# A row softmax on one core: 16-row tiles, four-row blocks in a fixed order, and stores from ScalarE's queue

## The chip, the cores and the metric

The kernel runs on one core of a Trainium2 chip. The metric is device time in microseconds (us), lower is better. One run in the profiler gives the trace; its span (first to last instruction) is about 2 us shorter than the measured time. Engines are named as in the profile: DVE is VectorE, ACT is ScalarE, POOL is GpSimd, SP is SyncE; a trailing q (ACTq) is an engine's sequencer, which hands work to the engine and issues DMAs. The input is 33.55 MB, the output is 33.55 MB.

## The reference

```python
x = np.random.randn(16, 1024, 512).astype(np.float32)

def reference(x):
    x_scaled = x / 0.5
    x_max = np.max(x_scaled, axis=-1, keepdims=True)
    exp_x = np.exp(x_scaled - x_max)
    return (exp_x / np.sum(exp_x, axis=-1, keepdims=True)).astype(np.float32)
```

That is 16384 independent softmaxes of 512 numbers each, after a multiplication by 2.

## The kernel before

A tile is 128 partitions by `G = 8` rows of 512 numbers (2 MB); there are 16 tiles and 8 buffers. The tile is changed in place and stored. The order of instructions on each engine is left to the framework's scheduler.

```python
G = 8
N_ACT_NORM = 2
xr   = xf.rearrange("(c p g) d -> c p g d", p=P, g=G)
outr = of.rearrange("(c p g) d -> c p g d", p=P, g=G)
data  = ctx.enter_context(tc.tile_pool(name="data", bufs=8))
stats = ctx.enter_context(tc.tile_pool(name="stats", bufs=8))

for c in range(C):                                   # C = 16
    xt = data.tile([P, G, D], fp32, name="xt")
    nc.sync.dma_start(out=xt, in_=xr[c])                              # L44, load
    nc.vector.reduce_max(negmax, xt, axis=AX, negate=True)            # L47
    for g in range(G):
        nc.scalar.activation(out=xt[:, g, :], in_=xt[:, g, :], func=EXP,   # L51
                             bias=negmax[:, g : g + 1], scale=2.0,
                             accum_out=sums[:, g : g + 1])
    nc.vector.reciprocal(recip, sums)                                 # L61
    k = N_ACT_NORM
    nc.vector.tensor_mul(xt[:, k:, :], xt[:, k:, :],                  # L65, six rows
                         recip[:, k:].unsqueeze(2).broadcast_to((P, G - k, D)))
    for g in range(N_ACT_NORM):                                       # L71, two rows
        nc.scalar.activation(out=xt[:, g, :], in_=xt[:, g, :], func=COPY,
                             scale=recip[:, g : g + 1])
    nc.gpsimd.dma_start(out=outr[c], in_=xt)                          # L78, store
# ... allocations of the small tiles and the launch are cut
```

The bias is `-max(x)` and not `-2 max(x)`; the constant cancels in the division.

The softmax here doesn't subtract the row's maximum and nothing guards it: scores larger than these inputs give would overflow.

Of the kernel before, what the change touches and what calls it, by code (L numbers as in the profile page):

```python
# [1 line left out]

# [4 lines left out]


@with_exitstack  # L10
def kernel(
    ctx: ExitStack,
    tc: tile.TileContext,
    x: bass.AP,
    out: bass.AP,
):
    nc = tc.nc
    fp32 = mybir.dt.float32
    P = nc.NUM_PARTITIONS

    D = x.shape[-1]
    xf = x.flatten_outer_dims()
    of = out.flatten_outer_dims()
    N = xf.shape[0]

    G = 8
    C = N // (P * G)
    assert C * P * G == N

    N_ACT_NORM = 2  # L30

    xr = xf.rearrange("(c p g) d -> c p g d", p=P, g=G)
    outr = of.rearrange("(c p g) d -> c p g d", p=P, g=G)

    data = ctx.enter_context(tc.tile_pool(name="data", bufs=8))
    stats = ctx.enter_context(tc.tile_pool(name="stats", bufs=8))

    AX = mybir.AxisListType.X
    EXP = mybir.ActivationFunctionType.Exp
    COPY = mybir.ActivationFunctionType.Copy  # L40

    for c in range(C):
        xt = data.tile([P, G, D], fp32, name="xt")
        nc.sync.dma_start(out=xt, in_=xr[c])  # L44

        negmax = stats.tile([P, G], fp32, name="negmax")
        nc.vector.reduce_max(negmax, xt, axis=AX, negate=True)  # L47

        sums = stats.tile([P, G], fp32, name="sums")
        for g in range(G):  # L50
            nc.scalar.activation(  # L51
                out=xt[:, g, :],
                in_=xt[:, g, :],
                func=EXP,
                bias=negmax[:, g : g + 1],
                scale=2.0,
                accum_out=sums[:, g : g + 1],
            )

        recip = stats.tile([P, G], fp32, name="recip")  # L60
        nc.vector.reciprocal(recip, sums)  # L61

        if N_ACT_NORM < G:
            k = N_ACT_NORM
            nc.vector.tensor_mul(  # L65
                xt[:, k:, :],
                xt[:, k:, :],
                recip[:, k:].unsqueeze(2).broadcast_to((P, G - k, D)),
            )
        for g in range(N_ACT_NORM):  # L70
            nc.scalar.activation(  # L71
                out=xt[:, g, :],
                in_=xt[:, g, :],
                func=COPY,
                scale=recip[:, g : g + 1],
            )

        nc.gpsimd.dma_start(out=outr[c], in_=xt)  # L78


# [1 line left out]
_INS = ['x']  # L82
_OUTS = [((16, 1024, 512), 'float32')]


# [23 lines left out]
```

## Time and profile before

| | before |
|---|---|
| time, median of 3 runs | 164.66 us (164.35 to 164.81) |
| span of the profiled run | 162.7 us |
| busy: DMA queues q1 + q0, DVE, ACT | 97.5%, 77%, 69% |
| rate in a steady stretch | 431 GB/s |

These are lines of the page of the kernel before: busy time per engine; the span in 40 slices of 4.07 us (DMA busy in tenths, and what the DMA engines moved); the DMA queues (packets, MB, share of the 16 DMA engines); and the costliest groups of instructions (busy us and mean ns of one, then the idle time before them).

```profile
span 162.7 us, 483 instructions
DVE 124.6 (77%) x48; ACT 112.5 (69%) x289; POOL 8.8 (5%) x20
DMA  5999999999999999999999999999999999979994
GB/s 161 431 431 427 431 439 334 411 433 443 423 423 443 431 419 443 439 415 439 443 411 433 443 423 423 443 431 419 439 443 415 435 443 415 431 318 447 407 431 193
q1 hardware_dynamic: 2304, 33.56, 49.2%
q0 software_dynamic: 2304, 33.56, 48.3%
q14 instruction: 2, 0.02, 0.0%
...
L51 ACT ACTIVATE xt<-xt,negmax 128x512 f32<-128x512 f32 x128 | 90.5, 708 | 28.3 <-DVE negmax L47 28.3
L47 DVE TENSOR_REDUCE negmax<-xt 128x8 f32<-128x4096 f32 x16 | 70.5, 4406 | 25.6 <-DMA xt<-in_x_dram 25.6
L65 DVE TENSOR_TENSOR xt<-xt,recip 128x3072 f32<-128x3072 f32 x16 | 53.6, 3349 | 0.1
```

The DMA engines are the only ones that work all the time. DVE and ACT have idle time, and what ends it is a load (DVE) or DVE (ACT). The rate is flat except in four places: the first slice, slice 7 (334 GB/s), slice 36 (318 GB/s), and the last. While the bytes and the steady rate stay the same, they are the only time that a change can win.

The view of stretches gives the same for chosen stretches of the kernel before (from:to and length in us, busy us and instructions of DVE, ACT and POOL, clock, DMA share, GB/s):

```profile
core 0: us, DVE busy (x) ACT busy (x) POOL busy (x), PEclk, DMA share, GB/s
24.40:28.50 4.10, 4.10 (x3) 2.98 (x8) 0.00 (x0) 1.00 1.00 332
48.00:136.00 88.00, 71.67 (x29) 66.63 (x173) 5.32 (x10) 1.00 1.01 431
142.00:146.50 4.50, 4.47 (x3) 4.50 (x13) 0.53 (x1) 1.00 0.82 350
146.50:152.00 5.50, 4.71 (x3) 2.73 (x6) 0.53 (x1) 1.00 0.95 396
```

The second dip is at 142 to 152 us. The timeline of DVE and of POOL's store issues, kernel before (start us, length us, engine, line, what; in brackets the idle time before it and what ended it):

```profile
134.36 0.20 DVE L61 RECIPROCAL recip<-sums 128x8 f32<-128x8 f32 x1
136.47 4.42 DVE L47 TENSOR_REDUCE negmax<-xt 128x8 f32<-128x4096 f32 x1 [1.91 <-DMA xt<-in_x_dram]
140.80 3.35 DVE L65 TENSOR_TENSOR xt<-xt,recip 128x3072 f32<-128x3072 f32 x1
...
134.99 0.53 POOL L78 DMA_DIRECT2D out_dram<-xt  x1 [9.18 <-ACT xt L51]
144.69 0.53 POOL L78 DMA_DIRECT2D out_dram<-xt  x1 [9.17 <-ACT xt L51]
```

At 134.36 us DVE has the reciprocals of tile 13 (counting from 0) and could multiply. But its next instruction is the reduction of tile 15, which waits 1.9 us for that tile's load and takes 4.4 us. The multiply starts at 140.80, and tile 13's store is issued at 144.69, 9.7 us after the one before. A 2 MB store alone takes about 4.9 us, so with the loads over the queue runs dry. While loads still run, they fill the same gap.

### The profile page before, as it was taken

To read this page: it belongs to the slowest core of one execution; us is meant where nothing else is said; L and a number is where in the kernel's file an instruction comes from. 1 tells how busy PE (TensorE), PEld (TensorE's weight loads), DVE (VectorE), ACT (ScalarE), POOL (GpSimd) and SP (SyncE) were. 2 spreads that over 40 slices of the span, in tenths; PEclk is the share of its full clock that TensorE was granted. 3 is DMA by queue.
4 is the path that set the end of the run, shared out by engine and by line. 5 is a ranking of instruction groups with operands and counts; after the bars stand their busy time and mean duration, and the time that the engine had idled before them with its cause. 6 is when DMAs were issued, how large, how long until landed. Compare 5 with 4: busy or idle time off the path is not lost.

```text
span 162.7 us, 483 instructions
## 1 busy us (share of the span) xinstructions
DVE 124.6 (77%) x48; ACT 112.5 (69%) x289; POOL 8.8 (5%) x20
## 2 busy tenths in 40 slices
DVE  0098799999999979596993959969596895999200
ACT  0038997999999995939589294885939579396000
POOL 0000010010101010101001010010101001011100
DMA  5999999999999999999999999999999999979994
GB/s 161 431 431 427 431 439 334 411 433 443 423 423 443 431 419 443 439 415 439 443 411 433 443 423 423 443 431 419 439 443 415 435 443 415 431 318 447 407 431 193
DMA packets 4610, 67.13 MB, mean 413 GB/s; under 512 B 512, under 2 KB 512, under 8 KB 512
## 3 DMA queue, kind: packets, MB, share of 16 engines
q1 hardware_dynamic: 2304, 33.56, 49.2%
q0 software_dynamic: 2304, 33.56, 48.3%
q14 instruction: 2, 0.02, 0.0%
HBM read 33.55 MB, written 33.55 MB: 413 GB/s over the span
## 4 chain that ended last, share of the span: by engine, by line
DMA 61%; DVE 18%; ACT 8%; issue 6%; POOLq 0%; SPq 0%
DMA xt<-in_x_dram 40%; DMA out_dram<-xt 22%; DVE negmax L47 11%; ACT xt L51 7%; DVE xt L65 6%; ACT xt L71 1%; DVE recip L61 0%; POOLq L104 0%; SPq L44 0%; POOLq L78 0%
## 5 line engine op out<-in xcount | busy, mean ns | idle before, releaser
L51 ACT ACTIVATE xt<-xt,negmax 128x512 f32<-128x512 f32 x128 | 90.5, 708 | 28.3 <-DVE negmax L47 28.3
L47 DVE TENSOR_REDUCE negmax<-xt 128x8 f32<-128x4096 f32 x16 | 70.5, 4406 | 25.6 <-DMA xt<-in_x_dram 25.6
L65 DVE TENSOR_TENSOR xt<-xt,recip 128x3072 f32<-128x3072 f32 x16 | 53.6, 3349 | 0.1
L51 ACT ACTIVATION_READ_ACCUMULATOR xt<-xt,negmax 128x1 f32 x128 | 24.0, 187 | 0.0
L71 ACT ACTIVATE xt<-xt,recip 128x512 f32<-128x512 f32 x32 | 21.1, 707 | 0.3 <-DVE recip L61 0.3
L78 POOL DMA_DIRECT2D out_dram<-xt x16 | 8.6, 540 | 143.5 <-ACT xt L51 89.3
L51 ACT ACT_TABLE_LOAD x1 | 1.3, 1283 | 8.4 <-DMA xt<-in_x_dram 8.4
L61 DVE RECIPROCAL recip<-sums 128x8 f32<-128x8 f32 x16 | 3.1, 195 | 1.2 <-ACT xt L51 1.2
L93 POOL MEMSET const-float32-0.0<- 128x1 f32 x1 | 0.1, 98 | 0.2 <-issue 0.2
L93 POOL MEMSET const-bfloat16-1.0<- 128x1 bf16 x1 | 0.1, 101 | 0.0
L93 POOL MEMSET const-float32-1.0<- 128x1 f32 x1 | 0.1, 98 | 0.0
L93 POOL MEMSET const-uint8-127<- 128x1 uint8 x1 | 0.1, 98 | 0.0
## 6 DMA issues: line engine op xcount, KB each, us to landing
xt<-in_x_dram SPq DMA_DIRECT2D x16, 2048.0 KB, 28.8
out_dram<-xt POOLq DMA_DIRECT2D x16, 2048.0 KB, 17.0
```

The lines of the kernel that those rows point to most:

```text
L47: nc.vector.reduce_max(negmax, xt, axis=AX, negate=True)
L51: nc.scalar.activation(out=xt[:, g, :], in_=xt[:, g, :], func=EXP, bias=negmax[:, g : g + 1], scale=2.0, accum_out=sums[:, g : g + 1],)
L61: nc.vector.reciprocal(recip, sums)
L65: nc.vector.tensor_mul(xt[:, k:, :], xt[:, k:, :], recip[:, k:].unsqueeze(2).broadcast_to((P, G - k, D)),)
L71: nc.scalar.activation(out=xt[:, g, :], in_=xt[:, g, :], func=COPY, scale=recip[:, g : g + 1],)
L78: nc.gpsimd.dma_start(out=outr[c], in_=xt)
L93: nc = _bacc.Bacc("TRN2", target_bir_lowering=False, num_devices=1)
```

## The change

Its intent: bigger transfers; compute that starts early, in blocks of four rows, with the stages of successive blocks in a fixed order on each engine; a multiply with one tensor source on DVE; no GpSimd in the loop. The core of the diff, with allocations cut:

```diff
-    G = 8
+    G = 16
+    B = 4
+    N_ACT = 1
-    N_ACT_NORM = 2
-    data = ctx.enter_context(tc.tile_pool(name="data", bufs=8))
+    FIRST = [(0, 4), (4, 16)]                       # tile 0 comes in two loads
+    data = ctx.enter_context(tc.tile_pool(name="data", bufs=6))
+    ctx.enter_context(tc.manual_schedule())         # order as written
+    nc.vector.memset(warm, 0.0)
+    nc.scalar.activation(out=warm, in_=warm, func=EXP)   # primes the table
...
-        nc.vector.reduce_max(negmax, xt, axis=AX, negate=True)
+        nc.vector.tensor_reduce(negmax, xb, axis=AX, op=MAX, negate=True)   # xb: 4 rows
+        nc.vector.tensor_scalar_mul(bias, negmax, 2.0)
...
-            nc.vector.tensor_mul(xt[:, k:, :], xt[:, k:, :], recip[:, k:]...broadcast)
+        for g in range(B - N_ACT):
+            nc.vector.tensor_scalar_mul(xb[:, g, :], xb[:, g, :], recip[:, g : g + 1])
...
-        nc.gpsimd.dma_start(out=outr[c], in_=xt)
+        if b + B == G:
+            nc.scalar.dma_start(out=outr[c], in_=tiles[c])
...
+    for i in range(n + 3):                          # n = 32 blocks
+        if i < n:
+            if blocks[i][1] == 0:
+                load(blocks[i][0])
+            shift(i)                                # DVE: reduce, double
+            exponentials(i)                         # ACT
+        if 1 <= i <= n:
+            scale_vector(i - 1)                     # DVE: reciprocal, 3 multiplies
+        if 2 <= i <= n + 1:
+            scale_scalar(i - 2)                     # ACT: 1 COPY
+        if 3 <= i:
+            store(i - 3)                            # ACT's queue, once per tile
```

More of the change, by code (lines that the diff above doesn't have):

```diff
@@ L19 @@
     P = nc.NUM_PARTITIONS
+    AX = mybir.AxisListType.X
+    EXP = mybir.ActivationFunctionType.Exp
+    COPY = mybir.ActivationFunctionType.Copy
+    MAX = mybir.AluOpType.max
     D = x.shape[-1]
@@ L24, with load, shift, exponentials @@
     N = xf.shape[0]
-    G = 8
+    G = 16
+    B = 4
+    N_ACT = 1
     C = N // (P * G)
     assert C * P * G == N
-    N_ACT_NORM = 2
     xr = xf.rearrange("(c p g) d -> c p g d", p=P, g=G)
     outr = of.rearrange("(c p g) d -> c p g d", p=P, g=G)
-    data = ctx.enter_context(tc.tile_pool(name="data", bufs=8))
-    stats = ctx.enter_context(tc.tile_pool(name="stats", bufs=8))
-    AX = mybir.AxisListType.X
-    EXP = mybir.ActivationFunctionType.Exp
-    COPY = mybir.ActivationFunctionType.Copy
-    for c in range(C):
-        xt = data.tile([P, G, D], fp32, name="xt")
-        nc.sync.dma_start(out=xt, in_=xr[c])
-        negmax = stats.tile([P, G], fp32, name="negmax")
-        nc.vector.reduce_max(negmax, xt, axis=AX, negate=True)
-        sums = stats.tile([P, G], fp32, name="sums")
-        for g in range(G):
+    FIRST = [(0, 4), (4, 16)]
+    data = ctx.enter_context(tc.tile_pool(name="data", bufs=6))
+    stats = ctx.enter_context(tc.tile_pool(name="stats", bufs=6))
+    ctx.enter_context(tc.manual_schedule())
+    warm = stats.tile([P, 1], fp32, name="warm", bufs=1)
+    nc.vector.memset(warm, 0.0)
+    nc.scalar.activation(out=warm, in_=warm, func=EXP)
+    tiles = {}
+    blocks = [(c, b) for c in range(C) for b in range(0, G, B)]
+    state = {}
+    def load(c):
+        xt = tiles[c] = data.tile([P, G, D], fp32, name="xt")
+        for lo, hi in FIRST if c == 0 else [(0, G)]:
+            nc.sync.dma_start(out=xt[:, lo:hi, :], in_=xr[c][:, lo:hi, :])
+    def shift(i):
+        c, b = blocks[i]
+        xb = tiles[c][:, b : b + B, :]
+        negmax = stats.tile([P, B], fp32, name="negmax")
+        nc.vector.tensor_reduce(negmax, xb, axis=AX, op=MAX, negate=True)
+        bias = stats.tile([P, B], fp32, name="bias")
+        nc.vector.tensor_scalar_mul(bias, negmax, 2.0)
+        state[i] = (xb, bias)
+    def exponentials(i):
+        xb, bias = state[i]
+        sums = stats.tile([P, B], fp32, name="sums")
+        for g in range(B):
             nc.scalar.activation(
-                out=xt[:, g, :],
-                in_=xt[:, g, :],
+                out=xb[:, g, :],
+                in_=xb[:, g, :],
                 func=EXP,
-                bias=negmax[:, g : g + 1],
+                bias=bias[:, g : g + 1],
                 scale=2.0,
@@ L58, with scale_vector, scale_scalar, store @@
             )
-        recip = stats.tile([P, G], fp32, name="recip")
+        state[i] = (xb, sums)
+    def scale_vector(i):
+        xb, sums = state[i]
+        recip = stats.tile([P, B], fp32, name="recip")
         nc.vector.reciprocal(recip, sums)
-        if N_ACT_NORM < G:
-            k = N_ACT_NORM
-            nc.vector.tensor_mul(
-                xt[:, k:, :],
-                xt[:, k:, :],
-                recip[:, k:].unsqueeze(2).broadcast_to((P, G - k, D)),
-            )
-        for g in range(N_ACT_NORM):
-            nc.scalar.activation(
-                out=xt[:, g, :],
-                in_=xt[:, g, :],
-                func=COPY,
-                scale=recip[:, g : g + 1],
-            )
-        nc.gpsimd.dma_start(out=outr[c], in_=xt)
+        for g in range(B - N_ACT):
+            nc.vector.tensor_scalar_mul(xb[:, g, :], xb[:, g, :], recip[:, g : g + 1])
+        state[i] = (xb, recip)
+    def scale_scalar(i):
+        xb, recip = state[i]
+        for g in range(B - N_ACT, B):
+            nc.scalar.activation(
+                out=xb[:, g, :], in_=xb[:, g, :], func=COPY, scale=recip[:, g : g + 1]
+            )
+    def store(i):
+        c, b = blocks[i]
+        if b + B == G:
+            nc.scalar.dma_start(out=outr[c], in_=tiles[c])
+    n = len(blocks)
+    for i in range(n + 3):
[10 more added lines that the diff above has]
+            store(i - 3)
 _INS = ['x']
```

## The prediction

> **What bounds the kernel now: the DMA engines.** In the page's 40 slices DMA stands at 9 in all but the first and last, near 431 GB/s; ScalarE (ACT) is busy 69%, VectorE (DVE) 77% of the span. 67.11 MB must move whatever the kernel does: at 431 GB/s that is 155.7 us of a 162.7 us span. The Trainium skill, "DMA: Bandwidth & Descriptors", section "Where 436 GB/s comes from", gives a fabric ceiling of 435 GB/s; the trace agrees (430 to 433 GB/s in every steady stretch, loads alone or mixed). The other 7 us, by the view of stretches: about 2.9 us before the first byte, 2.2 after the last, 1.0 at 24 to 28 us (the first software-queue store ramps slowly: 332 GB/s), 1.0 at 142 to 152 us (350 and 396 GB/s: store 14 is done before the last tiles are normalised).
>
> **What the change removes, adds and moves.**
> - ACT's work per row stays: one exponential per 0.706 us, one COPY of 0.615 us per four rows; 3.44 us per block, 110 us in all. Eight store issues join its queue, an estimated 0.35 to 0.65 us each (the sync queue's load issues took 0.33 to 0.64).
> - DVE: the reduction stays 0.55 us a row; the broadcast multiply (0.558 us a row) becomes one-source multiplies. The skill, "VectorE: DVE Perf Modes", section "The perf-mode tier table", gives fp32 one-source ops the 2x mode; no run yet shows it; I estimate 0.34 to 0.42 us. With reciprocal (0.2 us) and doubling, a block costs an estimated 3.6 to 3.9 us, 115 to 125 us in all.
> - So a 16-row tile costs 14 to 16 us of compute and 19.5 us of traffic: DMA stays the bound.
> - Bytes are unchanged. Stores move to ACT's hardware queue; the first issues near 37 to 40 us, not 22.8. The software ramp (1 us) should vanish.
> - Priming the exponential table and splitting the first load bring compute's start from 12.8 to about 8 us, off the DMA path.
>
> **How much is critical.** Only holes in DMA activity: about 2 us. A new hole is possible but not expected: the last store is 4.19 MB (9.7 us), and needs four blocks (14 to 16 us) and some 3 us of drain after the last load. I estimate that load lands at 121 to 124 us with equal sharing, the last store issues near 142, and earlier stores keep the DMA busy until about 149: 5 us of slack or more. Six buffers let loads 6 and 7 issue near 58 and 78 us, long before the load queue empties.
>
> **Prediction.** Span 160.5 to 161 us; measured time 162.8 us (span plus the 2 us by which the times exceed the profile before), 1.1% less. Range 161.3 to 166.0. Chances: faster by over 2% 0.10, within 2% 0.82, slower by over 2% 0.08.
>
> **What would show each step.** Right: DMA at 9 and about 431 GB/s in all slices but the ends; no dip at 24 to 28 us; DVE and ACT 70 to 78% busy; chain of waits mostly DMA; multiplies of 0.34 to 0.42 us. Wrong: a DMA hole between 125 and 152 us (last compute exposed), or a steady rate off 431 GB/s.
>
> **What would make it wrong.** (1) Loads getting less than half the bandwidth: at 46% the last load lands late enough to cost about 6 us. (2) Store issues that block ACT's queue for microseconds. (3) Another rate with 32 KB rows per partition or two hardware queues; 2% faster needs about 434 GB/s. (4) DVE at 0.56 us per multiply: slack is eaten, a few us at the end.

## The result, and the profile after

| | before | after |
|---|---|---|
| time, median | 164.52 us (4 runs, 164.35 to 164.81) | 163.01 us (4 runs, 162.92 to 163.27) |
| span of the profiled run | 162.7 us | 161.2 us |

The ratio is 0.9913, 95% interval 0.9888 to 0.9937: 0.9% less time, clear of noise and far below 2%. A ratio is the mean time of one kernel's fast runs over that of the other's fast runs of the same rounds, so it is not quite the ratio of the medians quoted. A run counts as slow when it takes over 1.5% more than the fastest of its kernel; slow runs are not compared.

The same parts of the page, now of the changed kernel (slices of 4.03 us):

```profile
span 161.2 us, 563 instructions
DVE 119.7 (74%) x193; ACT 114.8 (71%) x290; POOL 0.2 (0%) x4
DMA  5999999998999999999999999999999999999991
GB/s 193 457 463 447 390 463 447 392 455 317 417 472 398 431 472 398 423 480 398 423 472 409 390 488 423 390 488 423 390 488 423 390 488 425 390 480 431 390 480 65
q1 hardware_dynamic: 1296, 33.56, 49.2%
q10 hardware_dynamic: 1152, 33.55, 48.2%
q14 instruction: 4, 0.03, 0.0%
...
L74 ACT ACTIVATE xt<-xt,bias 128x512 f32<-128x512 f32 x128 | 90.8, 710 | 28.9 <-DVE bias L67 28.9
L65 DVE TENSOR_REDUCE negmax<-xt 128x4 f32<-128x2048 f32 x32 | 73.0, 2281 | 19.8 <-DMA xt<-in_x_dram 19.8
L89 DVE TENSOR_SCALAR xt<-xt,recip 128x512 f32<-128x512 f32 x96 | 40.9, 483 | 1.1
```

The DMA row is at 9 nearly everywhere, as before. The GB/s row swings more, because packets are now 32 KB and a slice counts whole packets by their start; the mean is what counts. The dip of slice 36 is gone. A dip when the first store begins is still there, now in slice 10 (317). The instruction queue q14 has fetched four times and not twice. The same stretches of the changed kernel:

```profile
48.00:136.00 88.00, 76.10 (x124) 72.03 (x184) 0.00 (x0) 1.00 1.00 433
142.00:146.50 4.50, 1.46 (x4) 2.47 (x5) 0.00 (x0) 1.00 1.03 444
146.50:152.00 5.50, 0.00 (x0) 0.00 (x0) 0.00 (x0) 1.00 0.93 399
158.00:161.20 3.20, 0.00 (x0) 0.00 (x0) 0.00 (x0) 1.00 0.07 31
```

The last line matters. From 158.0 us on only 31 GB/s times 3.2 us, about 0.1 MB, is left to start, yet the span goes on for 3.2 us. A few of the 16 DMA engines are late.

To see all terms at once I added up the trace's DMA records, spreading each packet's bytes evenly over its recorded time. "Lost" is DMA time lost against the kernel's own steady rate (52 to 132 us). "Median" and "last" are when the middle and the last of the 16 DMA engines report the end of their share of the last store. The experiments below are in the table too, except e5, e6 and e11.

```
                   rate   bytes/  lost:  lost:  lost:   median  last    last -  span    q14
                   GB/s   rate    start  first  132 to  engine  engine  median          fetches
                          us      0-8us  store  158us   us      us      us      us
before             431.2  155.6   2.9    1.0    1.2     160.7   160.9   0.15    162.7    2
after              432.7  155.1   2.4    1.0    0.0     158.3   160.0   1.60    161.2    4
e1_sw_stores       433.0  155.0   2.5    0.9    0.0     158.3   159.6   1.29    161.4    4
e2_plain_start     432.4  155.2   2.6    1.0    0.0     158.6   159.8   1.23    161.1    4
e3_before_ordered  431.1  155.7   2.9    0.5    0.0     159.1   159.8   0.71    161.6    2
e4_copy_only       433.3  154.9   2.5    0.9    0.0     158.3   158.7   0.36    159.8    0
e7_extra_instr     432.3  155.2   2.5    0.8    0.0     158.3   161.5   3.19    162.9   10
e8_fewer_instr     432.6  155.1   2.5    0.8    0.0     158.3   159.7   1.42    160.9    3
e9_after_again     433.0  155.0   2.5    1.0    0.0     158.4   160.0   1.64    161.3    4
e10_extra_reduce   432.8  155.1   2.5    1.2    0.8     159.6   160.2   0.59    161.4    4
e12_wide_blocks    433.1  155.0   2.7    0.8    0.0     158.4   159.4   0.98    160.6    2
```

"bytes/rate" plus the three losses gives the median engine within about 0.2 us. From before to after the median engine ends 2.4 us earlier: about 1.2 from the closed hole, 0.5 from a slightly higher rate, 0.5 from a quicker start (0.2 is left over). The rate goes with the 16-row tiles (e1 and the copy e4 have it, e3 does not; the number of buffers changed with them and was not separated); what made the start quicker was not separated. But the last engine ends only 0.9 us earlier, because the engines, in step before (0.15 us), are 1.6 us apart after. Another 0.5 us comes at the very end: from the last engine's report to the end of the span it takes 1.8 us with software stores (before, e1, e3) and 1.1 to 1.3 us in the other rows of the table. In total the span falls by 1.5 us.

### The profile page after: what moved, and what is told of

Read it like the earlier page. It is cut to its first block, busy times and chain, and to the rows that moved or that the text cites. A ratio compares the mean times of both kernels' runs of the same rounds, so it can differ in the third digit from the quotient of the medians.

```text
span 161.2 us, 563 instructions
## 1 busy us (share of the span) xinstructions
DVE 119.7 (74%) x193; ACT 114.8 (71%) x290; POOL 0.2 (0%) x4
## 4 chain that ended last, share of the span: by engine, by line
DMA 54%; DVE 31%; ACT 3%; issue 1%; SPq 0%
DMA xt<-in_x_dram 36%; DVE negmax L65 19%; DMA out_dram<-xt 18%; DVE xt L89 10%; ACT xt L74 2%; DVE bias L67 1%; ACT xt L95 1%; DVE recip L87 1%; SPq L59 0%
## 5 line engine op out<-in xcount | busy, mean ns | idle before, releaser
L74 ACT ACTIVATE xt<-xt,bias 128x512 f32<-128x512 f32 x128 | 90.8, 710 | 28.9 <-DVE bias L67 28.9
L65 DVE TENSOR_REDUCE negmax<-xt 128x4 f32<-128x2048 f32 x32 | 73.0, 2281 | 19.8 <-DMA xt<-in_x_dram 19.8
L89 DVE TENSOR_SCALAR xt<-xt,recip 128x512 f32<-128x512 f32 x96 | 40.9, 483 | 1.1
L74 ACT ACTIVATION_READ_ACCUMULATOR xt<-xt,bias 128x1 f32 x128 | 23.9, 187 | 0.0
L95 ACT ACTIVATE xt<-xt,recip 128x512 f32<-128x512 f32 x32 | 22.4, 706 | 0.0
L87 DVE RECIPROCAL recip<-sums 128x4 f32<-128x4 f32 x32 | 5.5, 171 | 1.6 <-ACT xt L74 1.6
L67 DVE TENSOR_SCALAR bias<-negmax 128x4 f32<-128x4 f32 x32 | 5.5, 170 | 1.1
```

The lines of the kernel that those rows point to most:

```text
L65: nc.vector.tensor_reduce(negmax, xb, axis=AX, op=MAX, negate=True)
L67: nc.vector.tensor_scalar_mul(bias, negmax, 2.0)
L74: nc.scalar.activation(out=xb[:, g, :], in_=xb[:, g, :], func=EXP, bias=bias[:, g : g + 1], scale=2.0, accum_out=sums[:, g : g + 1],)
L89: nc.vector.tensor_scalar_mul(xb[:, g, :], xb[:, g, :], recip[:, g : g + 1])
L95: nc.scalar.activation(out=xb[:, g, :], in_=xb[:, g, :], func=COPY, scale=recip[:, g : g + 1])
```

## The experiments

Each of the three groups of four ran on one chip with 5 rounds, beside 11 runs of the kernel before. That kernel has two modes of its own: of the 37 runs of it in all, 13 lie at 163.69 to 164.03 us and 24 at 164.27 to 164.95. So I compare medians of the variants with each other as well as ratios. What made the two modes was not looked at. The profiled run of the kernel before (span 162.7 us) is one of the slower mode, so all terms of the table above are counted from that mode. The spans of the faster mode, 161.5 to 161.9 us, are those of e3, in which the hole is closed; perhaps the hole does not open in that mode, but no trace of such a run was kept. Against the faster mode (median 163.83 us) the changed kernel wins 0.8 us, not 1.5.

### The store queue undone

```diff
-            nc.scalar.dma_start(out=outr[c], in_=tiles[c])
+            nc.gpsimd.dma_start(out=outr[c], in_=tiles[c])
```

> The changed kernel with its stores issued from GpSimd's software queue again, nothing else. Theory A (the DMA engines stall for about 1 us when the first store begins, whichever queue issues it; the gain of the change lies elsewhere): the dip near 35 to 40 us stays about 1 us, the time is 163.0 to 163.6 us, at most 0.4 us lost to a slightly lower rate when stores run alone. Rival (as predicted: the dip belongs to the software queue and the hardware queue would remove it): the dip is clearly larger here than in the changed kernel, and about 1 us comes back, 164.0 us or more.

Measured: 163.25 us (6 runs, 163.06 to 163.89), ratio to before 0.9941. Loss at the first store: 0.9 us against 1.0 in the changed kernel. So the dip is not the software queue's. The change of queue moved the median by 0.24 us or less (the control e9 on another chip has 163.21), which is within the noise here. The Trainium skill says in "DMA: Bandwidth & Descriptors", section "Issuing engines are not separate DMA queues", that issuing from another engine only saves the sequencer's issue time; this run agrees.

### The early start undone

```diff
-    FIRST = [(0, 4), (4, 16)]
+    FIRST = [(0, 16)]
-    warm = ...; nc.vector.memset(warm, 0.0); nc.scalar.activation(out=warm, in_=warm, func=EXP)
```

> The changed kernel without the primed table and with tile 0 loaded in one piece: compute starts near 15 us instead of 8. Theory A (only DMA holes count): 163.0 us, within 0.3 us of the changed kernel, the first store some 3 to 4 us later. Rival (earlier compute is part of the gain): 164 us or more.

Measured: 162.87 us (5 fast runs; a sixth, slow, took 165.45), ratio 0.9913. The first store is issued at 37.6 us, not 34.2, and the time is the same. Starting compute earlier is worth nothing here.

### The kernel before with only the order fixed

```diff
+    ctx.enter_context(tc.manual_schedule())
+    for c in range(C + 1):
+        if c < C:
+            head(c)          # load, reduce_max, exponentials of tile c
+        if c >= 1:
+            tail(c - 1)      # reciprocal, multiply, COPYs, software store of tile c-1
```

> The kernel before with nothing changed but the order: reduction of tile c, then the multiply of tile c-1, fixed on each engine (8-row tiles, 8 buffers, one broadcast multiply and software stores kept). Theory A (about 1.1 us of the gain is the hole at 144 to 152 us, made by the multiply of tile c standing behind the reduction of tile c+2): the hole goes, span near 161.5, time 163.3 to 163.7 us against 164.5 for before. Rival (the gain comes from tile size, buffers or queue): no change, 164.5 us.

Measured: 163.86 us (6 runs, 163.66 to 164.04), ratio 0.9971, interval 0.9944 to 0.9998. The hole is closed. The same two stretches of this run, to set against 350 and 396 GB/s before:

```profile
142.00:146.50 4.50, 2.15 (x3) 4.50 (x12) 0.53 (x1) 1.00 1.01 433
146.50:152.00 5.50, 1.46 (x1) 0.29 (x1) 0.53 (x1) 1.00 1.00 429
```

The order that does it, on DVE, and the store of tile 13 on POOL, in this run:

```profile
128.73 0.19 DVE L65 RECIPROCAL recip<-sums 128x8 f32<-128x8 f32 x1
128.96 3.36 DVE L67 TENSOR_TENSOR xt<-xt,recip 128x3072 f32<-128x3072 f32 x1
134.13 4.42 DVE L49 TENSOR_REDUCE negmax<-xt 128x8 f32<-128x4096 f32 x1 [1.82 <-DMA xt<-in_x_dram]
...
136.12 0.53 POOL L79 DMA_DIRECT2D out_dram<-xt  x1 [9.18 <-ACT xt L73]
```

Now the multiply of tile 13 comes before the reduction of tile 15, which still waits for its load, and the store is issued at 136.12 us, not 144.69. So the order alone, without a single other part of the change, closes the hole. The expected time, 163.3 to 163.7, was a little too good. The median DMA engine ends 1.6 us earlier (160.7 to 159.1), of which 0.5 us is a smaller loss at the first store (0.5 us, not 1.0; why was not looked at) and 1.2 us the hole. The last engine ends only 1.1 us earlier: the hole had brought the engines into step, and without it they end 0.7 us apart (e10, below, shows a hole doing this). The time fell by 0.5 to 0.7 us (ratio, medians), and by nothing against the faster mode of the kernel before.

### No compute at all

```diff
-    (memset, table, shift, exponentials, scale_vector, scale_scalar, schedule)
+    for c in range(C):
+        xt = data.tile([P, G, D], fp32, name="xt")
+        (loads of tile c as before)
+        nc.scalar.dma_start(out=outr[c], in_=xt)
```

> Loads and stores of the changed kernel with no compute between (result wrong on purpose: it copies x). Theory A (both kernels sit on the DMA floor): 162 to 163 us, at most 1 us under the changed kernel, and the same dip of about 1 us when the first store begins, now near 10 to 15 us. Rival (compute is still exposed somewhere in the changed kernel): 160 us or less.

Measured: 161.66 us (6 runs, 161.28 to 162.09); the result is wrong, on purpose. That is the floor of these transfers: the changed kernel is 1.35 us above it, 0.8%. I had expected at most 1 us. The table says where the rest is: rate, start, first store and median engine are those of the changed kernel; the difference is that the engines end 0.36 us apart and not 1.6. No packet of data starts after 158 us (the last column, GB/s, is 0):

```profile
158.00:159.80 1.80, 0.00 (x0) 1.00 0.01 0
```

The dip at the first store is here too (0.9 us at 13 to 21 us), with no compute in the kernel. So it belongs to the DMA traffic itself.

### Is the dip paid once, by the first write?

```diff
+    scratch = dram.tile([P, 128], fp32, name="scratch")      # in DRAM
+    nc.vector.memset(seed, 0.0)
+    nc.scalar.dma_start(out=scratch, in_=seed)               # e5; nc.gpsimd in e6
```

> The changed kernel with one extra store of 64 KB to a scratch DRAM tensor, issued from ScalarE's queue near 1 us, before any load data moves. Theory B (the stall of about 1 us, with 3 to 5 us between issue and first byte, belongs to the first store of the program and is paid once): the dip near 36 to 40 us is gone, the first real store moves bytes within 2 us of its issue, span about 160.2, time near 162.0 us. Rival (the stall comes with the first large mixing of loads and stores): dip unchanged, 163.0 us.

> As the run above, with the scratch store issued from GpSimd's software queue, while the real stores stay on ScalarE's. If the stall is paid by the first write to DRAM, whichever queue: dip gone, near 162.0 us. If it is paid by the first use of a queue: dip unchanged, 163.0 us.

Measured: 163.21 us (163.01 to 163.83) and 163.47 us (163.21 to 163.79). The dip stays: the first store is issued at 34.6 us in e5, its first bytes move at 38.9, and 0.8 us is lost. Theory B falls in both forms. What makes the first store take 4 to 5 us to begin, and slows the loads meanwhile, stays open; it is neither the kind of queue nor a first write to DRAM or on that queue.

### Do instruction fetches hold up single DMA engines?

```diff
+    for _ in range(768):
+        nc.gpsimd.memset(dust, 0.0)          # e7: [128, 1], GpSimd is otherwise idle
```

> The changed kernel with 768 one-column memsets on the idle GpSimd engine: no work for the DMA engines but 48 KB of instructions, some 6 fetches more of 8 KB. Theory C (the 16 DMA engines, in step in the copy-only run, finish up to 1.6 us apart because instruction fetches hold up single engines): more fetches on the instruction queue, the last store's engines finish further apart, 0.5 to 2 us more time. Rival (the skew has another cause): 163.0 us.

Measured: 164.70 us (6 runs, 164.43 to 164.91), 1.5 us more than the control e9 (on another chip) and than e5 (163.21 us, on the same chip), and slower than before (ratio 1.0032). The page's line of the instruction queue in this run:

```profile
q14 instruction: 10, 0.08, 0.1%
```

Six more fetches of 8 KB. The median engine ends at 158.3 us as in the changed kernel; the last ends at 161.5, 3.2 us behind it. The reverse:

```diff
-        nc.vector.tensor_scalar_mul(bias, negmax, 2.0)
-        for g in range(B - N_ACT):
-            nc.vector.tensor_scalar_mul(xb[:, g, :], xb[:, g, :], recip[:, g : g + 1])
+        nc.vector.tensor_mul(xb[:, :k, :], xb[:, :k, :], recip[:, :k]...broadcast)   # e8, k = 3
```

> The changed kernel with one broadcast multiply per block instead of three, and without the doubled bias: VectorE has 97 instructions, not 193, and is slower per block (about 4.0 us, not 3.79). Theory C: 2 fetches instead of 4, less skew at the end, 162.4 to 162.8 us. Theory A (VectorE is off the critical path) and no theory C: 163.0 us. Rival (the cheaper multiplies were part of the gain): 163.5 us or more.

Measured: 162.75 us (6 runs, 162.42 to 163.76), with three fetches, not the two expected, and engines 1.4 us apart. DVE is busier (81% against 74%), and the time is not longer (ratio 0.9923, against 0.9927 for the control). Over all runs without a hole in the last 26 us, the distance from the median to the last engine is 0.4 us with 0 fetches, 0.7 to 1.0 with 2, 1.4 with 3, 1.2 to 1.6 with 4 and 3.2 with 10. One fetch is recorded as a single packet of 309 ns. The records don't name its engine, but the landings in the traces show what follows it: each load or store reports 16 times, which I take as once per engine. So many us behind the middle of the 16 came the four latest:

```
                          landing   fetches   four latest engines
                          near us   so far    us behind the middle
e4, last store            158.7     0         0.07  0.08  0.11  0.37
e7, first load              5.2     0         0.09  0.12  0.13  0.19
e7, second load            12.5     1         0.10  0.11  0.15  0.60
e7, third load             22.3     1         0.10  0.11  0.14  0.60
e7, fourth load            32.0     2         0.10  0.11  0.57  0.64
e7, last store            158.7     10        0.80  1.58  1.80  3.25
after, last store         158.7     4         0.56  0.95  1.47  1.67
```

The first two fetches of e7, at 11.2 and 31.4 us, are each followed by one more engine that is about 0.4 us later than it was. Between them, while the memsets go on, nothing moves. In eight other runs a fetch at 30 to 32 us is followed by the same: at the landing near 32 us one engine is 0.3 to 0.7 us later than it was. So the delay comes with the fetch and not with the memsets; and at the end four engines are late, not one. Not all of the lag is so plain: in e12, which fetches nothing between 31.7 and 93.4 us, the last engine falls back from 0.6 us (41.9 us) to 2.3 us (65.5 us) after the first store begins, and is 1.0 us late once the loads are over (120 us). In the copy-only run, where no engine was late before the first store, none falls more than 0.4 us behind. What enlarges a lag there stays open.

### How much compute time is hidden?

> The changed kernel itself, unaltered, as the control on this chip beside the three runs below. 163.0 us, within 0.3 us; 4 instruction fetches, engines of the last store up to 1.6 us apart.

The control: 163.21 us (6 runs, 163.04 to 163.35), as expected. Beside it:

```diff
+        nc.vector.tensor_reduce(again, xb[:, :1, :], axis=AX, op=MAX, negate=True)   # e10
```

> The changed kernel with one more one-row reduction per block on VectorE (result unused): 0.55 us more per block, 4.34 us. Theory A with the slack read from the trace (last store issued at 144.5 us, the one before it leaves the DMA engines near 148.9): VectorE now runs without a pause from 12.7 us, 31 blocks of 4.34 us end near 147 us, the last store issues near 150 to 151 us, the DMA engines stand idle for 2 to 4 us, time 165.0 to 167.0 us. Rival (compute has much more slack, or none was there): 163.0 us, or over 168 us.

Measured: 163.47 us (6 runs, 163.24 to 163.54). The expectation failed. A block cost 4.26 us, not 4.34, and the last store was issued at 148.2 us, not 150 to 151: just in time, for there is no hole behind it. The store before it was late instead, issued at 139.2, and left a hole; the stretches of this run:

```profile
136.00:139.00 3.00, 3.00 (x4) 2.46 (x7) 0.00 (x0) 1.00 0.83 360
139.00:142.00 3.00, 2.96 (x7) 2.83 (x8) 0.00 (x0) 1.00 0.85 360
```

The hole cost the median engine 1.2 us (159.6 against 158.4 in the control) but the last engine only 0.15 us, and the time 0.26 us. In the hole the engines that are ahead stand idle, and those that lag catch up: they end 0.6 us apart, not 1.6. So in this run a late hole that was smaller than the lag was nearly free. The kernel before shows the same at its own hole: its last engine reported 0.80 us behind the middle one before it (store landing at 145.3 us) and 0.09 us behind after it (151.2 us). This is why closing that hole gave back so little.

### The last store in four pieces

```diff
+        if c == C - 1:
+            nc.scalar.dma_start(out=outr[c][:, b : b + B, :], in_=tiles[c][:, b : b + B, :])
```

> The changed kernel with the last tile stored in four 1 MB pieces, each when its block is done. Theory A (earlier stores keep the DMA engines busy until 149 us, so nothing is waiting for the last store): 163.0 us, within 0.3 us. Rival (the last 4 MB store is exposed): 162 us or less.

Measured: 163.35 us (6 runs, 163.16 to 163.64), 0.14 us above the control. The last 4 MB store is not exposed.

### A version that beats both

```diff
-    B = 4
-    N_ACT = 1
+    B = 8
+    N_ACT = 2
-    FIRST = [(0, 4), (4, 16)]
+    FIRST = [(0, 8), (8, 16)]
     (one broadcast multiply and no doubled bias, as in e8; store(i - 2) in place of store(i - 3))
```

> The changed kernel with its tiles, buffers, queue and fixed order, but with blocks of 8 rows, one broadcast multiply per block and no doubled bias: 49 VectorE instructions, not 193, and the same ScalarE count. Theory C: 2 instruction fetches as before, less skew than with 4, 162.3 to 162.8 us, faster than both kernels. If only compute structure mattered: 163.5 us or more.

Measured: 162.58 us (6 runs, 162.36 to 163.20), ratio to before 0.9895, interval 0.9871 to 0.9919, against 163.21 for the control on the same chip. From its page:

```profile
span 160.6 us, 419 instructions
DVE 125.4 (78%) x49; ACT 113.0 (70%) x290; POOL 0.2 (0%) x4
q14 instruction: 2, 0.02, 0.0%
```

It uses the old compute (blocks of 8 rows, one broadcast multiply) in the new frame (16-row tiles, fixed order, ACT's queue). DVE is busier than in the changed kernel, and the kernel is faster. Its median engine ends when the control's does (158.4 us), its last one 0.6 us earlier.

## Why the prediction was right

The prediction was 162.8 us, range 161.3 to 166.0, "within 2%"; measured 163.01 (span 161.2, just above the predicted 160.5 to 161). Point by point:

- **DMA is the bound: right.** The copy without compute takes 161.66 us; the changed kernel is 0.8% above it. Later compute (e2), slower DVE (e8) and one more reduction per block (e10) made the time longer by at most 0.3 us.
- **"155.7 us for the bytes": right.** At the measured steady rates it is 155.6 before and 155.1 after. The ceiling of 435 GB/s that the Trainium skill gives, "DMA: Bandwidth & Descriptors", section "Where 436 GB/s comes from", is not crossed: 431 to 433 in all runs. The same section says that for transfers between HBM and SBUF a limit of HBM, about 358 GB/s per core, binds before that; here, with one core at work, it did not.
- **The hole at 142 to 152 us closes: right, and shown by the order alone (e3).** My words for its cause ("store 14 is done before the last tiles are normalised") missed the mechanism and were one store off: the multiply of tile 13 stands behind the reduction of tile 15.
- **"The software ramp (1 us) should vanish": wrong.** The loss is 1.0 us before and 1.0 us after. It is there with software stores (e1, 0.9), with no compute (e4, 0.9) and after a primed write (e5, 0.8); only e3, with 8-row tiles and software stores, loses less (0.5).
- **Its place in the sum was filled by terms that I had not listed:** a quicker start (2.9 to 2.4 us lost), a rate 0.4% higher (0.5 us), and 0.5 us less after the last engine's report. Against these stands a term that I had not listed either: the engines end 1.6 us apart, not 0.15. My 2 us of holes came out as 1.5 us of span by this offsetting, not by a correct list: that the number came so close is luck.
- **DVE's multiply at 0.34 to 0.42 us: right.** Three take 1.28 us in the timeline, one 483 ns with overlap, so about 0.40 us apart, against 0.558 us a row before. The skill's "VectorE: DVE Perf Modes", section "The perf-mode tier table", gives such an instruction (`tensor_scalar`) the 2x mode for fp32; not every operation with one source has it, as the prediction's words suggest (`tensor_reduce` stays at 1x there). This trace shows a gain of 1.4 times per row at 512 elements, fixed costs included. It won nothing: e8 and e12 undo it; e8 is no slower and e12 is faster.
- **Compute's start at 8 us, off the DMA path: right.** The first exponential starts at 7.96 us, and e2 shows that the start is worth nothing.
- **A block at 3.6 to 3.9 us: right** (3.79 in the timeline).
- **First store at 37 to 40 us: wrong,** it was at 34.2, harmlessly. The sequencer issues the store when its semaphores allow, while ACT still has queued work in front of it. The timeline of ACT, changed kernel:

```profile
33.24 0.70 ACT L95 ACTIVATE xt<-xt,recip 128x512 f32<-128x512 f32 x1
34.20 0.72 ACT L74 ACTIVATE xt<-xt,bias 128x512 f32<-128x512 f32 x1 [0.25 <-DVE bias L67]
34.23 0.37 ACTq L102 DMA_DIRECT2D out_dram<-xt  x1
```

  In the program the store comes after four exponentials and one COPY of the next blocks, and it is issued as soon as the first of them starts.
- **Last store near 142, needed by 149: right in kind.** It was issued at 144.5 us; the DMA engines come to it about 9.7 us before the median end of 158.3, near 148.6. So the slack is 4 us, not 5 or more. Cutting that store up (e11) wins nothing.

## What to carry to other kernels

When the DMA engines are busy throughout, a new compute structure can win little more than the holes in their activity, so measure the floor first with a copy that does the same transfers. In a fixed order on one engine, do not let work that releases a store fall behind work that waits for a much later load: two tiles later opened the hole here, one tile later (e3) closed it. Once the holes are closed the slowest of the 16 DMA engines sets the end, and there fewer instructions beat faster ones (e12).

## What the Trainium skill lacked or had wrong

- "Runtime: NRT & Kernel Launch", section "Instruction fetch mechanics", has instruction memory refilled in blocks of 16 KiB and calls the cost mostly hidden. The trace shows fetches of 8 KB, and in a DMA-bound kernel they show in the time: six more moved the last DMA engine from 1.6 to 3.2 us behind the median and cost 1.5 us.
- "DMA: Bandwidth & Descriptors", section "Specifications", gives a first-byte latency of about 1 us for the software path and 0.6 us for the hardware path. With loads queued, the first store moved its first byte 5.0 us (software, 22.8 to 27.8) and 4.4 us (hardware, 34.2 to 38.6) after its issue (the first load, with nothing queued, 1.0 us: 0.74 to 1.75), and the loads lost 1 us of DMA time meanwhile. I found this on no page.
